# Gated DeltaNet: the first pass's front in 24 fixed slots, and the steps of the triangular inverse 2.7 slots later in each stretch

## The chip, the cores and the metric

The kernel runs on one core of a Trainium2 chip. The metric is device time in microseconds (us), the median of the runs. TensorE (PE in the profile) does the matrix products, VectorE (DVE), ScalarE (ACT) and GpSimd (POOL) do the rest, and SyncE (SP) issues the DMA transfers. Each engine works through its own list of instructions in order.

## The reference, cut to what matters

One inference step of a trunk of two layers: gated DeltaNet (layer 0), then RWKV-7 (layer 1), over 1,104 token rows (64 sample rows, 16 meta tokens, 1,024 prompt tokens). The change touches layer 0 alone. Its core, for each of 16 value heads:

```
proj = xn @ w_in                                  # k, q, v, z and the gate inputs b, a
q, k, v = silu(causal_conv(qkv));  q, k = l2norm(q), l2norm(k)
beta = sigmoid(b);  g = -exp(a_log) * softplus(a + dt_bias);  gc = cumsum(g)
decay = exp(gc[i] - gc[j])                        # causal
L = strict_lower((k*beta) @ k.T * decay);  A = L + I
u, wk = solve(A, v*beta), solve(A, k*beta*exp(gc))      # triangular
v_new = u_c - wk_c @ S                            # chunk after chunk
o = (q*exp(gc)) @ S + (q @ k.T * decay) @ v_new
S = S * exp(g_last) + k_dec.T @ v_new             # state to the next chunk
out = (rmsnorm(o, gn_w) * silu(z)) @ w_out
```

## The kernel before, in words

Layer 0 goes through eight passes j = 0 to 7, each with one key head and its two value heads. A pass has a *front* and a *chain*.

The front makes what doesn't depend on the state: the products k, q and v (tiles `dk`, `dq`, `dv` on TensorE, of xa/xc with the split weights `whi` and `wlo`), the causal convolution (`cvy`, filter taps on DVE, line L520), the SiLU, keys `K`, queries `Q`, value rows `vt` and `bv`; the decay matrices `E` (read from `drow` in DRAM, then exponentials on ACT); the scores of keys with keys; and then the inverse of A. For the inverse the 32 x 32 diagonal blocks of the scores go through DRAM (`ltd`) into one tile of 72 partitions (`invA`); 31 *steps* of two DVE instructions each (`invtmp`, L567, and `invT`, L569) invert all blocks together. `spread` then copies the transposed result on ACT (`invA<-invT`, L737) and sends it through DRAM (`g_t`, `g_u`) into `T1n` (L743) and `TT` (L750). Four *merges* (`rY`, `rU` on TensorE) join blocks of 32 to 64 and to 128.

The chain (`gdn_recur`) takes the state `S` through nine token groups of three units each: `rA` products on TensorE, `X`, `w` and `o`, and the update `S` on DVE (L899). It reads the inverse `TT` of its own pass.

The products run in *slots* of 12 matmuls. A generator, `products()`, yields after each slot, and the 36 slots of a stretch hold k of pass j (6 slots), z of pass j−1 (12), q of pass j (6) and v of pass j (12). Everything else is an *event* with a slot number, put into a table by `gdn_events`, `chain_events` (chain of pass j, from slot `first[j]` on) and `front_events` (front of pass j, by `b` = its stretch's first slot, `qb` = b + 18, and `a` = `first[j]`). `before(u)` calls all events due before slot u. So the chain of pass j−1 and the front of pass j run in the same stretch. On TensorE and ACT the order of the program is the order of execution (`tc.manual_schedule`); on DVE, POOL and SP a scheduler orders the rows by priorities that follow the order of the program.

Before the change pass 0 is an exception: its gates, keys, queries, values, inverse and merges are written out one after the other ahead of slot 0, outside of the manual schedule, and the scheduler orders them on all engines.

The calls that the change speaks of, in `front_events`: `e` is the slot of the first decay, `k` that of the first scores; steps come two at a time in 16 slots from k + 6.6, `spread` at a − 10.3 and the merges at a − 6.5, −4.5, −3.5 and −1.5.

Of the kernel before, what the change touches and what calls it, by code (L numbers as in the profile page):

```python
# [35 lines left out]
class Builder:  # L36
# [308 lines left out]
    def gates(self, xh, xl):  # L345
# [25 lines left out]
        nc.vector.tensor_tensor_scan(gc, sm[32:48], g[32:48], 0.0, op0=ALU.mult, op1=ALU.add)  # L371
        gd = rows[64:80]
# [295 lines left out]
    def gdn_prep(self, j, G):  # L668

        nc, t, gp, fp = self.nc, self.t, self.gp, self.fp  # L670
# [246 lines left out]
    def gdn_events(self, G, open_):  # L917
# [68 lines left out]
    def front_events(self, j, G, b, qb, a, a0, open_):  # L986
# [9 lines left out]
        va, e = qb + 6, max(b + 0.3, a0 - 3.4)  # L996
        k = max(b + 5.5, e + 4.7)
        at(b - 5.7, open_, j)
        at(b - 1.4, lambda: self.history_turn(g().H))
        at(b + 0.1, lambda: self.gdn_prep(j, g()))  # L1000
        for s in range(3):
            at(e + 2 * s, lambda s=s: g().decay(s))
            for tt in range(3):
                at(k + 2 * s - 1.8 + 0.7 * tt, lambda s=s, tt=tt: g().exps(s, tt))
            at(k + 2 * s, lambda s=s: g().scores(s))
            at(qb + (7.6, 16.4, 20.4)[s], lambda s=s: self.gdn_query_norms(g(), s))
        at(k + 4.4, lambda: g().scales())
        at(k + 4.7, lambda: g().blocks())
# [5 lines left out]
        at(b + 11.8, lambda: self.gdn_sample_keys(g(), 0))  # L1014
        at(qb + 4.2, lambda: self.gdn_sample_keys(g(), 1))
        for h, q in ((0, 0), (0, 1), (1, 0)):
            at(b + 13.2, states, h, q)
        at(qb + 6.4, read, 0)
        at(qb + 6.5, states, 1, 1)
        at(qb + 9.9, read, 1)  # L1020
# [1084 lines left out]
    def layer0(self, top, right, xa, xc):  # L2105
# [22 lines left out]
        self.gates(kh, kl)  # L2128
# [6 lines left out]
        def rest(g):  # L2135
            for _ in g:
                pass
        open_(0)
        self.history_turn(G[0].H)
        rest(G[0].keys(0))  # L2140
        self.gdn_zero()
        gates.close()
        self.gp = pool("gdn", ctx)
        g = G[0]
        self.gdn_prep(0, g)
        for s in range(3):
            g.decay(s)
            for tt in range(3):
                g.exps(s, tt)
            g.scores(s)  # L2150
        g.scales()
        g.blocks()
        g.steps(31)
        g.spread()
        rest(self.gdn_queries(0, g, kh, kl, 2048))
        for x in (0, 1):
            self.gdn_sample_keys(g, x)
        for h in (0, 1):
            self.gdn_sample_read(g, h, [self.sample_states(0, h, q) for q in (0, 1)])
        for s in range(3):  # L2160
            self.gdn_query_norms(g, s)
        for h in (0, 1):
            dense = self.gdn_values(0, g, h, kh, kl, (2176, 1152)[h])
            for s in range(3):
                next(dense)
                next(dense)
                self.gdn_value_rows(g, h, s)
            rest(dense)
# [382 lines left out]
```

## Time and profile before

| | |
|---|---|
| median of 3 runs | 2245.91 us (2240.99 to 2247.82) |
| profiled execution: time, span, granted TensorE clock | 2250.41 us, 2248.7 us, 0.968 |
| busy: TensorE, DVE, ACT, POOL | 93%, 71%, 57%, 42% of the span |
| first slot (slot 0) begins | 112.2 us |
| first matmul of chain 0 | 171.5 us |
| a stretch of 36 slots (pass 4) | 526.58 to 652.27: 125.69 us |
| steps of the inverse, all passes (L567 and L569) | 101.3 + 91.3 us of DVE |

A row of a window gives its length, and for TensorE, its weight loads, DVE, ACT and POOL the busy time and the count of instructions, then the granted clock, the DMA share and GB/s. A row of waits gives the total, the times and the longest wait. A row of the timeline gives start, duration, engine, line, operation, output and inputs, shapes and count, and in square brackets the idle time ahead and what ended it. A row of a group ends with busy time, the mean of one in ns, and the idle time ahead of the group.

### The profile page before, as it was taken

The numbers are of one execution on the slowest core, as the hardware profiler recorded it, in microseconds if no ns is written. First come the engines' busy times: TensorE is split into PE (matmuls) and PEld (weight loads), VectorE is DVE, ScalarE is ACT, GpSimd is POOL, SyncE is SP. The second block draws the span as 40 slices with busy tenths as digits, with TensorE's granted clock in tenths as the row PEclk, the third lists the DMA queues.
The fourth block names the chain that finished last, engine by engine and source line by source line (L and its number), as shares of the span: only waits on it lengthen the run. The fifth ranks groups of instructions, "written<-read, shape, count | busy, mean of one in ns | idle before, by whom it ended". The sixth has DMA issues, their size and how long they took to land. (4 is left out here: it accounts for less than half of the span.)

```text
span 2248.7 us, 54824 instructions
## 1 busy us (share of the span) xinstructions
PE 2082.0 (93%) x20404; PEld 1934.5 (86%) x20404; DVE 1586.9 (71%) x4213; ACT 1271.9 (57%) x3641; POOL 941.9 (42%) x1253
## 2 busy tenths in 40 slices
PE   5869899999999999989899999979899999999997
PEld 5859898989898989989799999979798988788886
DVE  7866878788787878876323585676888747766755
ACT  5525556556465656556633365674746546677774
POOL 3533545445353534444323154244533344444444
PEclk9979999999999999999999999989999999999998
DMA  4413332333343333324525314645566375677764
GB/s 119 111 47 85 97 109 80 91 86 98 91 110 79 101 104 86 101 83 117 162 75 139 90 49 150 219 160 179 162 183 174 114 216 162 186 216 226 235 179 137
DMA packets 430661, 292.65 MB, mean 130 GB/s; under 512 B 147145, under 2 KB 412986, under 8 KB 430394
## 3 DMA queue, kind: packets, MB, share of 16 engines
q1 hardware_dynamic: 430394, 289.14, 44.8%
q8 instruction: 161, 2.64, 0.5%
q14 instruction: 106, 0.87, 0.1%
HBM read 197.68 MB, written 91.37 MB: 129 GB/s over the span
## 5 line engine op out<-in xcount | busy, mean ns | idle before, releaser
L90 POOL TENSOR_TENSOR wlo<-wraw,whi 128x512 fp32r<-128x512 f32 (+1 forms) x246 | 336.2, 1368 | 374.8 <-ACT whi L86 321.0
L76 PE MATMUL d<-xc,whi 128*128 128x384 f32 (+2 forms) x1006 | 279.9, 337 | 3.8 <-ACT whi L86 3.8
L520 DVE SCALAR_TENSOR_TENSOR cvy<-raw,cw,cvy 128x408 f32<-128x408 f32 (+2 forms) x288 | 192.1, 667 | 22.8 <-ACT cvy L62 20.6
L86 ACT CAST whi<-wraw 128x512 fp32r<-128x512 f32 (+1 forms) x246 | 149.9, 612 | 91.1 <-PE d L76 52.5
L76 PEld LDWEIGHTS d<-xc,whi 128*128 128x128 f32 (+1 forms) x1006 | 184.4, 190 | 6.0 <-ACT whi L86 4.2
L76 PE MATMUL d<-xc,wlo 128*128 128x384 f32 (+3 forms) x476 | 158.2, 341 | 2.8 <-POOL wlo L90 2.7
L76 PE MATMUL dz<-xc,whi 128*128 128x384 f32 (+1 forms) x480 | 154.8, 340 | 0.0
L76 PE MATMUL dv<-xc,whi 128*128 128x384 f32 (+1 forms) x480 | 152.3, 338 | 0.6 <-ACT whi L86 0.6
L76 PE MATMUL d<-xa,whi 128*128 128x384 f32 (+3 forms) x450 | 143.4, 343 | 3.9 <-DVE xb L1143 2.3
L1086 POOL TENSOR_SCALAR Sb<-Sb,eglb 128x128 f32<-128x128 f32 x128 | 105.3, 839 | 73.2 <-DVE X L877 34.4
L567 DVE TENSOR_TENSOR invtmp<-invA,invT 72x31 f32<-72x31 f32 (+15 forms) x248 | 101.3, 409 | 39.8 <-DMA invA<-ltd 36.0
L62 ACT ACTIVATE o<-rA,gcol 128x128 f32<-128x128 f32 x128 | 42.4, 367 | 147.2 <-DVE S L899 146.8
L76 PE MATMUL dz<-xa,whi 128*128 128x384 f32 (+1 forms) x288 | 99.7, 346 | 0.0
L76 PE MATMUL dv<-xa,whi 128*128 128x384 f32 (+1 forms) x288 | 98.7, 343 | 0.0
L76 PEld LDWEIGHTS d<-xc,wlo 128*128 128x128 f32 (+1 forms) x476 | 89.8, 190 | 7.0 <-POOL wlo L90 4.0
L76 PEld LDWEIGHTS dz<-xc,whi 128*128 128x128 f32 x480 | 90.0, 190 | 4.6 <-issue 4.5
L569 DVE TENSOR_TENSOR invT<-invT,invtmp 72x31 f32<-72x31 f32 (+15 forms) x248 | 91.3, 368 | 3.7
L76 PEld LDWEIGHTS d<-xa,whi 128*128 128x128 f32 (+1 forms) x450 | 85.8, 193 | 7.0 <-issue 4.3
L76 PEld LDWEIGHTS dv<-xc,whi 128*128 128x128 f32 x480 | 89.1, 188 | 2.5 <-issue 1.6
L76 PE MATMUL d<-xa,wlo 128*128 128x384 f32 (+3 forms) x252 | 86.4, 343 | 1.4 <-POOL wlo L90 1.4
L76 PE MATMUL rA<-S,K 128*128 128x128 f32 x256 | 52.1, 308 | 34.9 <-DVE S L899 26.1
L76 PEld LDWEIGHTS rA<-S,K 128*128 128x128 f32 x256 | 41.3, 200 | 44.6 <-DVE S L899 30.4
(523 smaller groups left out, 6963.6 us busy)
## 6 DMA issues: line engine op xcount, KB each, us to landing
wraw<-in_gdn_w_in SPq DMA_DIRECT2D x96, 256.0 KB
wraw<-in_rwkv_w_rkvz SPq DMA_DIRECT2D x80, 256.0 KB
Sb<-in_state_gdn SPq DMA_DIRECT2D x64, 256.0 KB
sldcak<-cakd SPq DMA_DIRECT2D x24, 576.0 KB
wraw<-in_rwkv_w_o SPq DMA_DIRECT2D x42, 256.0 KB
E<-drow SPq DMA_DIRECT2D x24, 384.0 KB
attn<-drow SPq DMA_DIRECT2D x24, 384.0 KB
wraw<-in_gdn_w_out SPq DMA_DIRECT2D x36, 256.0 KB
```

The costliest lines, as they stand in the source:

```text
L62: return self.nc.scalar.activation(out, in_, func, bias=bias, scale=scale, **kw)
L76: self.nc.tensor.matmul(out, lhsT, rhs, start=start, stop=stop)
L86: nc.scalar.copy(hi, x)
L90: e.tensor_tensor(lo, x, hi.bitcast(F32), op=ALU.subtract)
L520: nc.vector.scalar_tensor_tensor(y[0][:, 0:wd], raw[:, k:k + wd], cw[k], y[0][:, 0:wd], op0=ALU.mult, op1=ALU.add)
L567: nc.vector.tensor_tensor(tmp, A[:, j, j + 1:32].unsqueeze(2).broadcast_to([nb, n, m]), Tv[:, j, 0:m].unsqueeze(1).broadcast_to([nb, n, m] ...
L569: nc.vector.tensor_tensor(Tv[:, j + 1:32, 0:m], Tv[:, j + 1:32, 0:m], tmp, op=ALU.subtract)
L1086: self.nc.gpsimd.tensor_scalar(Sb[g][:, u], Sb[g][:, u], self.eglb[:, 2 * j + h, 4 * g + u:4 * g + u + 1], None, op0=ALU.mult)
```

## The change

Three things are changed, and what they compute stays the same.

1. The front of pass 0 gets 24 slots of its own, −24 to −1, within the manual schedule: `products()` begins with k, q and v of pass 0. `gates` becomes a generator whose five later pieces are events at −22.9, −19.4, −16.8, −16.7 and −16.6; decays, exponentials and scores of pass 0 lie at −18.5 to −13.6, its steps three to a slot from −11.5 on, `spread` at −1, and its merges by `first[0]`, as in the other passes.
2. `first` is 9, 43, 78, 114, … where it was 7, 43, 78, 114, …: chain 0 starts two slots later.
3. For the passes 1 to 7 the steps begin at k + 9.3 (15 slots, two steps each) where they began at k + 6.6 (16 slots), and `spread` is at a − 9.9 where it was at a − 10.3.

```diff
@@ gates
             self.act(ya, ya, AF.Exp, scale=-1.0)
+        yield
         xa, ya = x[32:48], y[32:48]
...
         nc.vector.tensor_tensor_scan(gc, sm[32:48], g[32:48], 0.0, op0=ALU.mult, op1=ALU.add)
+        yield
...
         for t3 in range(3):
+            yield
             p = self.ps("f", 2)
@@ gdn_events
-        first = [base[j + 1] + (7 if j < 2 else 6) for j in range(8)]
+        first = [9, 43] + [base[j + 1] + 6 for j in range(2, 8)]
+        for u in (-22.9, -19.4, -16.8, -16.7, -16.6):
+            self.at(u, gate)
+        self.at(-13, swap)
...
-                self.front_events(j, G, base[j], base[j] + 18, first[j], first[j - 1], open_)
+                self.front_events(j, G, base[j], base[j] + 18, first[j], open_, base[j] + max(0.3, first[j - 1] - base[j] - 3.4))
+            else:
+                self.front_events(0, G, -24, -18, first[0], None, None)
@@ front_events
+        if j:
...
+            inv, per, kk, ss, rd = [k + 9.3 + n for n in range(15)], 2, (b + 11.8, qb + 4.2), b + 13.2, (qb + 6.4, qb + 9.9)
+            sp = a - 9.9
+        else:
+            ed, ee, es = [-18.5, -18.4, -18.3], [-16, -15.2, -14.4], [-15.2, -14.4, -13.6]
+            inv, per, kk, ss, rd = [-11.5 + n for n in range(10)], 3, (-12.2, -12.1), -12.8, (-7.6, -4.1)
+            sp = -1
...
-        for n in range(16):
-            at(k + 6.6 + n, lambda: g().steps(2))
-        at(a - 10.3, lambda: g().spread())
+        for u in inv:
+            at(u, lambda: g().steps(per))
+        at(sp, lambda: g().spread())
@@ layer0
-        g.steps(31)
-        g.spread()
-        rest(self.gdn_queries(0, g, kh, kl, 2048))
...
-        for m in g.merges:
-            m()
-        self.last_tokens(0, g.H)
-        self.gdn_events(G, open_)
+        self.gdn_events(G, open_, lambda: next(gate, None), swap)
         def products():
+            yield from G[0].keys(0)
+            yield from self.gdn_queries(0, G[0], kh, kl, 2048)
+            yield from self.gdn_values(0, G[0], 0, kh, kl, 2176)
+            yield from self.gdn_values(0, G[0], 1, kh, kl, 1152)
...
-        before(0)
+        before(-24)
         with tc.manual_schedule(engines={mybir.EngineType.PE, mybir.EngineType.Activation}):
-            self.slot = 0
+            self.slot = -24
```

How the rows stand is best seen at three places. First ACT at the end of the front of pass 0, around the copy of `spread`. Before:

```order
L62 ACTIVATE cvy_1691<-raw_1651,cw_393 128x384
L62 ACTIVATE raw_1607<-cvy_1644 128x408
L86 CAST whi_1735<-wraw_1604 128x512
L544 COPY raw_1720<-dk_1722 128x336
L62 ACTIVATE cvy_1757<-raw_1720,cw_393 128x336
L62 ACTIVATE ktok_1764<-mktok_1762,gcol_123 128x128 x2
L62 ACTIVATE raw_1651<-cvy_1691 128x384
L737 COPY invA_808<-invT_810 72x1024
L62 ACTIVATE TT_11_115<-rU_1453 32x6x32 x2
```

The same place after:

```order
L62 ACTIVATE fss_1336,qeps_1005<-fss_1336 128x128 x3
L547 COPY raw_1317<-dv_1319 128x336
L740 COPY invA_923<-invT_925 72x1024
L62 ACTIVATE cvy_1383<-raw_1317,cw_393 128x336
L62 ACTIVATE raw_1234<-cvy_1293 128x384
L543 COPY raw_1402<-dk_1405 128x8x8
L544 COPY raw_1402<-dk_1405 128x320
L62 ACTIVATE cvy_1463<-raw_1402,cw_393 128x408
```

Before, the copy stood behind all filter work of pass 1's keys (`dk`). Now it stands ahead of the last filter rows of pass 0's own values (`cvy_1383`, and the SiLU `raw_1234`, whose result the next value rows on DVE and then transposes on TensorE take).

Second, DVE in the stretch of pass 4 (526.58 to 652.27 us), where the steps begin; `X`, `S` and `o` belong to the running chain of pass 3. Before:

```order
L877 SCALAR_TENSOR_TENSOR X_7360<-rA_7364,gcol_123,bv_6396 128x128
L1030 SCALAR_TENSOR_TENSOR ovar_7385<-ssq_6937,qeps_6134 128x6
L877 SCALAR_TENSOR_TENSOR X_7361<-rA_7365,gcol_123,bv_6396 128x128
L567 TENSOR_TENSOR invtmp_7339<-invA_7291,invT_7293 72x31
L569 TENSOR_TENSOR invT_7293<-invT_7293,invtmp_7339 72x31
L567 TENSOR_TENSOR invtmp_7342<-invA_7291,invT_7293 72x60
L569 TENSOR_TENSOR invT_7293<-invT_7293,invtmp_7342 72x30x2
L567 TENSOR_TENSOR invtmp_7393<-invA_7291,invT_7293 72x87
```

After:

```order
L880 SCALAR_TENSOR_TENSOR X_7354<-rA_7358,gcol_123,bv_6393 128x128
L1046 SCALAR_TENSOR_TENSOR ovar_7379<-ssq_6937,qeps_6116 128x6
L880 SCALAR_TENSOR_TENSOR X_7355<-rA_7359,gcol_123,bv_6393 128x128
L831 SCALAR_TENSOR_TENSOR zg_7399<-zg_7399,dz_7339 128x384
L110 TENSOR_TENSOR on_t_7382<-ors_7381 128x6
L111 SCALAR_TENSOR_TENSOR on_t_7382<-on_t_7382,ovar_7379 128x6
L112 SCALAR_TENSOR_TENSOR ors_7381<-on_t_7382,ors_7381 128x6
L902 SCALAR_TENSOR_TENSOR S_6936<-S_6936,eglb_124,rA_7358 128x128
L902 SCALAR_TENSOR_TENSOR S_6936<-S_6936,eglb_124,rA_7359 128x128
L570 TENSOR_TENSOR invtmp_7442<-invA_7291,invT_7293 72x31
L572 TENSOR_TENSOR invT_7293<-invT_7293,invtmp_7442 72x31
```

The two rows of `S` that follow `X` now stand ahead of the first step; before they stood behind the sixth.

Third, DVE in the same stretch where the steps end, near the last `S` of the chain. Before:

```order
L899 SCALAR_TENSOR_TENSOR S_6936<-S_6936,eglb_124,rA_7897 128x128
L520 SCALAR_TENSOR_TENSOR cvy_7938<-raw_7871,cw_393,cvy_7938 128x384
L899 SCALAR_TENSOR_TENSOR S_6936<-S_6936,eglb_124,rA_7898 128x128
L567 TENSOR_TENSOR invtmp_8005<-invA_7291,invT_7293 72x31
L910 TENSOR_TENSOR o_7892<-o_7892,rA_7897 128x128
L569 TENSOR_TENSOR invT_7293<-invT_7293,invtmp_8005 72x31
L910 TENSOR_TENSOR o_7892<-o_7892,rA_7898 128x128
```

After:

```order
L570 TENSOR_TENSOR invtmp_8085<-invA_7291,invT_7293 72x87
L572 TENSOR_TENSOR invT_7293<-invT_7293,invtmp_8085 72x3x29
L570 TENSOR_TENSOR invtmp_8088<-invA_7291,invT_7293 72x60
L902 SCALAR_TENSOR_TENSOR S_6936<-S_6936,eglb_124,rA_8011 128x128
L902 SCALAR_TENSOR_TENSOR S_6936<-S_6936,eglb_124,rA_8012 128x128
L572 TENSOR_TENSOR invT_7293<-invT_7293,invtmp_8088 72x2x30
L822 TENSOR_TENSOR bv_8116<-f_8117,sk_6637 128x3x128
L570 TENSOR_TENSOR invtmp_8147<-invA_7291,invT_7293 72x31
L913 TENSOR_TENSOR o_8006<-o_8006,rA_8011 128x128
L913 TENSOR_TENSOR o_8006<-o_8006,rA_8012 128x128
L572 TENSOR_TENSOR invT_7293<-invT_7293,invtmp_8147 72x31
```

Before, the last step stands behind the last but one update `S` of the chain (nine token groups; the last `S` follows 15 rows further on); now it stands behind the last one.

More of the change, by code (lines that the diff above doesn't have):

```diff
@@ L668, in gdn_prep @@
     def gdn_prep(self, j, G):
-        nc, t, gp, fp = self.nc, self.t, self.gp, self.fp
+        nc, t, fp = self.nc, self.t, self.fp
         col = self.col
@@ L995, in read @@
             self.gdn_sample_read(g(), h, [Sb[h, q] for q in (0, 1)])
[L996 to L999, printed above, removed]
+        va = qb + 6
         at(b + 0.1, lambda: self.gdn_prep(j, g()))
+        if j:
+            at(b - 5.7, open_, j)
+            at(b - 1.4, lambda: self.history_turn(g().H))
+            k = max(b + 5.5, e + 4.7)
+            ed, ee, es = [e + 2 * s for s in range(3)], [k + 2 * s - 1.8 for s in range(3)], [k + 2 * s for s in range(3)]
+            inv, per, kk, ss, rd = [k + 9.3 + n for n in range(15)], 2, (b + 11.8, qb + 4.2), b + 13.2, (qb + 6.4, qb + 9.9)
[4 more added lines that the diff above has]
+            sp = -1
@@ L1001, in front_events @@
         for s in range(3):
-            at(e + 2 * s, lambda s=s: g().decay(s))
+            at(ed[s], lambda s=s: g().decay(s))
             for tt in range(3):
-                at(k + 2 * s - 1.8 + 0.7 * tt, lambda s=s, tt=tt: g().exps(s, tt))
-            at(k + 2 * s, lambda s=s: g().scores(s))
+                at(ee[s] + (0.7 if j else 0.25) * tt, lambda s=s, tt=tt: g().exps(s, tt))
+            at(es[s], lambda s=s: g().scores(s))
             at(qb + (7.6, 16.4, 20.4)[s], lambda s=s: self.gdn_query_norms(g(), s))
-        at(k + 4.4, lambda: g().scales())
@@ L1015, in front_events @@
-        at(qb + 4.2, lambda: self.gdn_sample_keys(g(), 1))
+        at(kk[0], lambda: self.gdn_sample_keys(g(), 0))
+        at(kk[1], lambda: self.gdn_sample_keys(g(), 1))
         for h, q in ((0, 0), (0, 1), (1, 0)):
[L1017 to L1020, printed above, removed]
+            at(ss, states, h, q)
+        at(rd[0], read, 0)
+        at(rd[0] + 0.1, states, 1, 1)
+        at(rd[1], read, 1)
         for h in (0, 1):
@@ L2127, in layer0 @@
         rows = [xa[:, k] for k in range(6)] + [xc[:, k] for k in range(10)]
-        self.gates(kh, kl)
+        gate = self.gates(kh, kl)
+        next(gate)
         G = [None] * 8
@@ L2133, in open_, with swap @@
             G[j].H = self.history(j)
-        def rest(g):
-            for _ in g:
-                pass
+        def swap():
+            gates.close()
+            self.gp = pool("gdn", ctx)
         open_(0)
         self.history_turn(G[0].H)
-        rest(G[0].keys(0))
         self.gdn_zero()
[L2142 to L2152, printed above, removed]
-        g.steps(31)
-        g.spread()
-        rest(self.gdn_queries(0, g, kh, kl, 2048))
[L2156 to L2168, printed above, removed]
-        for m in g.merges:
-            m()
-        self.last_tokens(0, g.H)
-        self.gdn_events(G, open_)
+        self.gdn_events(G, open_, lambda: next(gate, None), swap)
         def products():
+            yield from G[0].keys(0)
+            yield from self.gdn_queries(0, G[0], kh, kl, 2048)
+            yield from self.gdn_values(0, G[0], 0, kh, kl, 2176)
+            yield from self.gdn_values(0, G[0], 1, kh, kl, 1152)
             for j in range(1, 8):
```

8 lines of the change are left out of this document (4 added, 4 removed).

## The prediction

> **What bounds the kernel now.** I read the page's first part, then the windows by stage, then who waits for whom, and last the order in time at the places where the change works.
>
> ```profile
> PE 2082.0 (93%) x20404; PEld 1934.5 (86%) x20404; DVE 1586.9 (71%) x4213; ACT 1271.9 (57%) x3641; POOL 941.9 (42%) x1253
> core 0: us, PE busy (x) PEld busy (x) DVE busy (x) ACT busy (x) POOL busy (x), PEclk, DMA share, GB/s
> 112.20:171.50 59.30, 38.94 (x375) 36.17 (x373) 39.40 (x99) 15.44 (x41) 21.12 (x27) 0.71 0.22 54
> 106.22:150.80 44.58, 30.41 (x150) 27.82 (x148) 39.91 (x103) 13.75 (x42) 22.91 (x27) 0.81 0.12 32
> 526.58:652.27 125.69, 119.33 (x1025) 112.83 (x1020) 102.16 (x279) 71.90 (x231) 54.95 (x82) 0.99 0.35 94
> 585.40:641.60 56.20, 50.20 (x370) 47.47 (x369) 49.85 (x136) 30.31 (x103) 27.81 (x40) 0.97 0.28 77
> 590.64:595.82 5.18, 4.94 (x21) 4.75 (x21) 4.96 (x15) 5.18 (x18) 1.28 (x1) 0.67 0.16 41
> 599.05:602.15 3.10, 3.10 (x22) 3.10 (x22) 2.23 (x8) 2.39 (x8) 0.39 (x2) 1.00 0.03 5
> 338.29:343.47 5.18, 4.94 (x20) 4.75 (x21) 4.67 (x16) 4.73 (x18) 0.00 (x0) 0.67 0.01 2
> ```
>
> TensorE is the bound (93%). A steady stretch of 36 slots (526.58:652.27) takes 125.69 us with 119.33 busy, so 6.36 us of it is idle. The end of the front (112.20:171.50) is the one place where TensorE is busy for only 38.94 of 59.30 us, at a granted clock of 0.71. So the change can win in two places: the front, once, and the idle time of the stretches, several times.
>
> The waits name the idle time; the first row below is for 460 to 1031 us (stretches j=3 to 7), the second for 182 to 460 (j=1 and 2), the third for the whole span.
>
> ```profile
> PE rA L76 <- DVE S L899: 20.4, 10, 5.0
> PE rA L76 <- DVE S L899: 5.7, 4, 1.9
> DVE invtmp L567 <- DMA invA<-ltd: 36.0, 8, 6.2
> ```
>
> The first and the third are one story, seen in order of time in the stretch j=4:
>
> ```profile
> 583.81 0.60 PE L76 MATMUL rA<-w,ktok 128*128 128x128 f32 x4
> 585.38 1.25 DVE L567 TENSOR_TENSOR invtmp<-invA,invT 72x31 f32<-72x31 f32 x1 [5.02 <-DMA invA<-ltd]
> 590.25 0.60 DVE L899 SCALAR_TENSOR_TENSOR S<-S,eglb,rA 128x128 f32<-128x128 f32 x2
> 590.64 0.49 PE L76 MATMUL rA<-S,K 128*128 128x128 f32 x2 [3.83 <-DVE S L899]
> 338.29 0.49 PE L76 MATMUL rA<-S,K 128*128 128x128 f32 x2 [1.60 <-DVE S L899]
> ```
>
> VectorE works in its order. Its first inverse step stands at the head and waits 5.02 us for the scores to come back from DRAM. Behind it stand six steps and then the state update S of the running chain, whose inputs were on TensorE at 583.81; S runs at 590.25 and TensorE waits 3.83 us for it. TensorE pays again: after the gap the clock is 0.67 for 5.18 us (590.64:595.82, 21 matmuls), while 22 matmuls take 3.10 us at clock 1.00 (599.05:602.15). I charge 5.18 − 3.10 = 2.1 us. The Trainium skill (TensorE: Matmul & The Clock Gate, "HAM oscillation — how this bites in real kernels") gives the rule "no PE-idle gaps >~3.4µs". By it the short gaps in j=1 and j=2 would cost no clock. The trace disagrees: the gap of 1.60 us at 338.29 is followed by the same 0.67 for 5.18 us (338.29:343.47). By the rule the sum would be about 2 us smaller (half of twice 2.1); I go by the rows.
>
> **The change part by part.**
>
> *Steps 2.7 slots later, stretches j=3 to 7.* In the new order of VectorE the S pair stands ahead of the first step. S could run at about 585.0 (583.81 plus its own matmuls), before the DMA lands at 585.38, so the wait no longer holds it. The possible gain of a stretch is 20.4 / 5 = 4.1 us of stall and 2.1 of clock: 6.2, for five stretches 31. It is not all there to have: the first step can't begin ahead of its transfer, all steps but one still stand ahead of the last S of the chain, and the window between the two gets shorter by whatever is gained.
>
> ```profile
> L567 DVE TENSOR_TENSOR invtmp<-invA,invT 72x31 f32<-72x31 f32 (+15 forms) x248 | 101.3, 409 | 39.8 <-DMA invA<-ltd 36.0
> L569 DVE TENSOR_TENSOR invT<-invT,invtmp 72x31 f32<-72x31 f32 (+15 forms) x248 | 91.3, 368 | 3.7
> 633.40 0.31 SPq L740 DMA_DIRECT2D g_t<-invT  x1
> 636.25 1.43 SPq L743 DMA_DIRECT2D T1n<-g_t  x3
> 641.65 0.61 DVE L899 SCALAR_TENSOR_TENSOR S<-S,eglb,rA 128x128 f32<-128x128 f32 x2 [1.52 <-PE rA L76]
> 643.46 2.13 ACT L737 COPY invA<-invT 72x1024 f32<-72x1024 f32 x1
> 651.02 1.33 PE L76 MATMUL rY<-T1n,E 32*32 32x32 f32 x72
> ```
>
> The steps of a pass cost (101.3 + 91.3) / 8 = 24.1 us. Before, the last one was over at 633.40 (the transfer of its result is issued there); now the last stands right behind S of 641.65. Between 585.40 and 641.60 VectorE is busy for 49.85 us. The first step's 1.25 us was a quarter of it work, and S itself moves ahead, so about 48.25 remain. TensorE's share of that window without stall and slow clock is 56.20 − 6.2 = 50.0. So VectorE would have to run at 96.5%. Where VectorE keeps today's idle time of 56.20 − 49.85 = 6.35 the stretch gains only 56.2 − 54.6 = 1.6 us; where its idle shrinks to 1.75 it gains 6.2. No row decides between them; most of its idle time now is waiting for TensorE, and that shrinks when TensorE doesn't stand. I take the middle, 3.9, times five: 19.5 us (ends 8 and 31).
>
> *Spread and merges.* Spread is issued 0.4 of a slot later; its ACT copy now waits for the last step at about 643.9, where it ran at 643.46 before. Its transfers of g_t, issued at 633.40 before, move to 643.9 and must be back as T1n before rY at 651.02. In the front the same path took (below) 156.39 − 150.78 = 5.6 us, so T1n is there at about 649.7: 1.3 us to spare. I charge nothing; the cover is that 1.3 us. Once it is gone, every later microsecond is a microsecond of TensorE, with 2.1 more for the clock. On SP's queue these DMAs move behind the state loads of that place, which are issued early; on POOL nothing moves past a step.
>
> POOL is the other neighbour: in the new place the steps lie beside its scaling of the sample states.
>
> ```profile
> 622.90 0.45 DVE L567 TENSOR_TENSOR invtmp<-invA,invT 72x175 f32<-72x175 f32 x1
> 623.50 2.43 POOL L1086 TENSOR_SCALAR Sb<-Sb,eglb 128x128 f32<-128x128 f32 x2
> 623.84 0.37 DVE L567 TENSOR_TENSOR invtmp<-invA,invT 72x156 f32<-72x156 f32 x1
> 627.72 1.29 POOL L90 TENSOR_TENSOR wlo<-wraw,whi 128x512 fp32r<-128x512 f32 x1 [1.78 <-ACT whi L86]
> 627.79 1.34 DVE L569 TENSOR_TENSOR invT<-invT,invtmp 72x112 f32<-72x112 f32 x1
> L1086 POOL TENSOR_SCALAR Sb<-Sb,eglb 128x128 f32<-128x128 f32 x128 | 105.3, 839 | 73.2 <-DVE X L877 34.4
> ```
>
> A step beside the scaling at 623.50 took its usual 0.37 us; only the one beside the weight split (627.79) was held, for about 1.0 us. The splits are as many as before, so no charge. The Trainium skill (GPSIMD Engine Reference, "Specifications") says that POOL shares its SBUF interfaces with VectorE and contends with instructions that read two SBUF inputs, as a step does; by it some nine more scalings beside steps, 0.84 us each, would cost VectorE up to 7.6 us a stretch and leave no gain there. The row at 623.84 speaks against it, so it only feeds the third case below.
>
> *j=1 and j=2.* The longest waits there are 1.9 and 1.6 us (the second at 338.29); with 2.1 of clock each that is about 8 in all. Half of it, as above: +4. Against it, chain 0 starts at slot 9 and chain 1 stays at 43, so in j=1 the last S and the merges are two slots nearer; the merges there may wait 2.5 us (between 0 and 5), and in j=2 0.5. Net +1.
>
> *The front of pass 0.* It had been placed by the scheduler; now slots −24 to −1 fix its products, gates and scores on TensorE and ACT.
>
> ```profile
> L520 DVE SCALAR_TENSOR_TENSOR cvy<-raw,cw,cvy 128x408 f32<-128x408 f32 (+2 forms) x288 | 192.1, 667 | 22.8 <-ACT cvy L62 20.6
> 95.01 1.64 DVE L706 SCALAR_TENSOR_TENSOR E<-fsc,bp,E 128x128 f32<-128x128 f32 x6
> 106.22 0.19 DVE L567 TENSOR_TENSOR invtmp<-invA,invT 72x31 f32<-72x31 f32 x1 [4.55 <-DMA invA<-ltd]
> 150.57 0.19 DVE L569 TENSOR_TENSOR invT<-invT,invtmp 72x31 f32<-72x31 f32 x1
> 150.79 1.93 ACT L737 COPY invA<-invT 72x1024 f32<-72x1024 f32 x1 [1.54 <-DVE invT L569]
> 150.78 0.30 SPq L740 DMA_DIRECT2D g_t<-invT  x1
> 156.39 2.71 PE L76 MATMUL rY<-T1n,E 32*32 32x32 f32 x72 [5.81 <-DMA T1n<-g_t]
> 179.88 0.34 PE L76 MATMUL dz<-xc,wlo 128*128 128x384 f32 x1
> 180.06 0.33 PE L76 MATMUL dz<-xc,whi 128*128 128x384 f32 x1
> 180.23 0.61 PE L76 MATMUL rA<-S,K 128*128 128x128 f32 x4
> ```
>
> Scores done at 96.65, first step at 106.22: a path of 9.6 us through DRAM. Then the steps last 44.58 us (106.22:150.80), though they are 24 us of work, because VectorE, busy for 39.91, does other rows among them. The new order has eight fewer of these ahead of the scores' end (four filter taps at 0.67 us, four others at the mean 39.91 / 103 = 0.39: 4.2 us) and sixteen fewer between the first and the last step (eight taps and eight others, 8.5 us). So the last step ends at 150.8 − 4.2 − 8.5 = 138.1 if VectorE is idle for as long as now, and at 133.4 if its 4.7 us of idle go; I take 136. What then stands behind it on TensorE? The transposes of the last value rows, since their SiLU stands behind the ACT copy: a visible wait of some 17 us (from about slot 2, at 122, to 140), longer than any now. From 136 to the end of slot 9: copy, filter and value rows 4.3; eight slots of 12 matmuls, seven at 2.13 (12 x 0.18, the distance of the dz rows) and one at the slow clock, 18.2; merges 7.2; small transposes 2.4; together 32.1, so 168. Before, slot 10 came at 180.23 with 3.7 us of chain work already in it, so 176.5 is its like. Gain 8.4, taken as 8. Ends: −5, where the new order's fixed rows make TensorE and ACT wait for gate pieces, each a chain over ACT, VectorE and DMA; +15, where most of the 17 us wait is filled.
>
> *Sum.* 19.5 + 1 + 8 = 28.5. The profiled execution took 2250.4 us (span 2248.7), so it would be 2222. The median of the runs is 2245.9, 4.5 lower: 2217.5; with a little for what the merges may lose I say 2219.
>
> **The rivals.** 0.3%, about what a measurement of this kernel can tell from no change, is 6.7 us.
>
> A, as forecast: gains of 16 to 38, so 2208 to 2230. Chance 0.50.
>
> B, VectorE has room enough and the stall goes whole: 31 + 1 to 5 + 8 to 12, so 2198 to 2206. For it speaks that VectorE's idle time is made of waits for TensorE; against it the 96.5%. Chance 0.18.
>
> C, VectorE becomes the bound between the first step and the last S: 1 us a stretch, 5, and a front of −1 to +10, so 2231 to 2242. For it speaks the sum of 48.25 in 50.0 us, and what the shared interface would add. Chance 0.14.
>
> D, slower: the steps end after the chain and T1n comes late. Each stretch then pays L − 1.3 for steps ending L later than the 643.9 above, and 2.1 for the clock, against its gain of 6.2. It decides at L of about 5.4; with the front's 8 us the whole kernel breaks even near L = 7. At L = 10, eight of the 24 us of steps behind the chain's S, each stretch loses 4.6, seven stretches 32 less the front's 8 and some of the small stalls: 2260 to 2270. Against it speaks that rows are ordered by slot, and the last step is listed right behind S. Chance 0.11.
>
> E, no change: the wait for the DMA only moves to another place of the same chain, and the front gives what it takes. 2240 to 2252. Against it speaks that S is ahead of the wait. Chance 0.07.
>
> **How the numbers follow.** Likeliest is A: 2219, its own range 2208 to 2230. The range 2198 to 2246 takes in B, C and most of E and leaves out D and tails, under 2 in 10. Faster: A, B and most of C, 0.79. Within 0.3%: most of E and the tail of C, 0.10. Slower: 0.11.
>
> **What the profile after would show.** The wait of rA for S falls from 20.4 us to under 5 in the stretches, which get 3 to 5 us shorter; the wait of invtmp for invA stays, with S ahead of it. A wait of about 17 us of a transpose f for vt in the front, and the first step near 102, the last near 136. If rY waits for T1n in each stretch, D is right; if S is late through all of the chain's second half, C. The prediction is wrong if the front loses: gate pieces that hold TensorE's row before slot −10 would show as waits of f or dq for ACT or VectorE.

## The result and the profile after

The changed kernel takes 2220.1 us (median of 4, 2219.3 to 2220.8), the kernel before 2245.9 (median of 4, 2241.0 to 2247.8): a ratio of 0.9871, interval 0.9849 to 0.9893. The forecast was 2219. The sum came out; its split did not, as the sections below show. One trace is of one execution: it took more than the median of its kernel by 10.4 us in late_steps, 8.7 in norm_late and 11.0 in spread_late, less by 11.9 in fold_before and 7.0 in fold_after, and lies within 5 us of it in the others.

The profiled execution after took 2219.6 us. The page's first lines, and three windows: the rest of the front (113.60:165.80), the stretch j=2 (258.25:390.46) and j=4 (516.77:640.65).

```profile
span 2217.4 us, 54821 instructions
PE 2061.5 (93%) x20404; PEld 1918.7 (87%) x20404; DVE 1572.4 (71%) x4213; ACT 1271.0 (57%) x3641; POOL 952.8 (43%) x1253
113.60:165.80 52.20, 33.93 (x397) 32.02 (x396) 34.66 (x84) 17.33 (x45) 16.53 (x30) 0.80 0.25 61
258.25:390.46 132.21, 123.35 (x1094) 117.39 (x1092) 99.57 (x282) 72.88 (x236) 62.88 (x84) 0.95 0.34 90
516.77:640.65 123.88, 118.51 (x1027) 112.52 (x1021) 96.97 (x279) 71.64 (x231) 57.06 (x82) 0.99 0.35 96
```

POOL is busy for 952.8 us where it was 941.9, with the same 1253 instructions: the one engine that got more expensive. The next table is made from the timelines: the time from the first `dk` matmul of one pass to that of the next, for all runs. "Loop" goes from the first product of pass 0 to the first `dz` behind the stretch j=7, "rest" from there to the end of the span (the last 24 slots with the chain of pass 7, then layer 1), where hardly a row is changed by any of them.

| run | pass 0 | j=1 | j=2 | j=3 | j=4 | j=5 | j=6 | j=7 | loop | rest |
|---|---|---|---|---|---|---|---|---|---|---|
| before | 66.0 | 159.2 | 127.5 | 127.7 | 125.7 | 126.0 | 126.0 | 126.6 | 984.7 | 1217.8 |
| control (before again) | 65.3 | 160.5 | 126.6 | 127.6 | 126.3 | 125.9 | 125.6 | 126.3 | 984.1 | 1215.5 |
| after | 68.3 | 144.7 | 132.2 | 126.3 | 123.9 | 122.7 | 121.8 | 123.8 | 963.7 | 1208.4 |
| late_steps | 66.7 | 162.2 | 131.6 | 130.1 | 124.1 | 124.7 | 124.1 | 122.5 | 986.0 | 1213.0 |
| front_only | 69.0 | 144.7 | 125.8 | 124.1 | 124.9 | 126.4 | 126.0 | 124.6 | 965.5 | 1205.7 |
| first7 | 68.1 | 150.2 | 131.5 | 127.7 | 121.0 | 123.9 | 122.0 | 123.9 | 968.3 | 1211.1 |
| norm_late | 69.1 | 145.2 | 132.6 | 123.6 | 120.5 | 121.4 | 123.3 | 123.4 | 959.2 | 1218.0 |
| mixed | 68.2 | 145.5 | 126.2 | 126.0 | 121.5 | 121.4 | 122.0 | 124.0 | 954.8 | 1203.0 |
| spread_late | 68.5 | 151.3 | 133.2 | 126.7 | 121.1 | 123.4 | 124.3 | 121.9 | 970.4 | 1214.6 |
| no_scaling | 69.3 | 139.9 | 129.6 | 119.9 | 118.0 | 118.7 | 118.4 | 118.1 | 932.1 | 1208.5 |
| fold_before | 66.9 | 155.2 | 124.8 | 123.9 | 120.5 | 121.4 | 120.5 | 119.9 | 953.2 | 1205.6 |
| fold_front_only | 68.2 | 138.5 | 124.8 | 122.6 | 121.8 | 120.5 | 119.9 | 121.2 | 937.5 | 1211.8 |
| fold_mixed | 68.4 | 138.0 | 124.9 | 123.9 | 119.3 | 119.1 | 119.0 | 119.0 | 931.6 | 1211.9 |
| fold_after | 67.9 | 140.5 | 124.4 | 121.0 | 119.4 | 119.1 | 119.1 | 119.2 | 930.5 | 1206.3 |

Two things are to be read from it. The rest varies between 1203 and 1218 us with nearly the same code, so the 9.4 us by which the two profiles differ there need not be the change's. And with the late steps the stretches j=4 to 7 are shorter than before by 1.3 to 5.2 us each, but j=2 is longer by 4 to 6, in every kernel of the upper nine that has them there.

The five stretches j=3 to 7 together, before and after:

```profile
398.91:1030.88 631.97, 599.89 (x5104) 567.46 (x5099) 502.69 (x1396) 359.38 (x1148) 272.94 (x408) 0.98 0.35 95
390.46:1009.02 618.56, 591.49 (x5104) 561.61 (x5100) 490.51 (x1396) 358.14 (x1148) 284.81 (x408) 0.99 0.35 97
```

They are 13.4 us shorter. For the same 5104 matmuls TensorE is busy for 8.4 us less, at a granted clock of 0.99 in place of 0.98, and idle for 5.0 us less. So the larger part came by the clock, the smaller by less idle time.

**Where the waits went.** In the stretches j=3 to 7 (after, 390 to 1009 us), TensorE's two largest waits and the largest of DVE:

```profile
PE rA L76 <- DVE S L902: 12.2, 10, 2.3
PE dv L76 <- POOL wlo L90: 8.2, 5, 1.8
DVE on_t L110 <- POOL ors L102: 27.8, 10, 5.4
```

The wait for S fell from 20.4 to 12.2 us, not to under 5. In the order of time, at the place of j=4 where DVE stood before for `invA`:

```profile
574.39 0.86 POOL L650 TENSOR_SCALAR_AFFINE_SELECT attn<-attn 128x768 f32<-128x768 f32 x1 [9.70 <-PE rA L76]
575.23 1.28 POOL L90 TENSOR_TENSOR wlo<-wraw,whi 128x512 fp32r<-128x512 f32 x1
576.47 1.33 POOL L102 TENSOR_TENSOR ors<-ovar,cvals 128x6 f32<-128x6 f32 x1
571.87 0.56 DVE L831 SCALAR_TENSOR_TENSOR zg<-zg,dz 128x384 f32<-128x384 f32 x1 [1.76 <-ACT zg L62]
577.83 0.17 DVE L110 TENSOR_TENSOR on_t<-ors 128x6 f32<-128x6 f32 x1 [5.41 <-POOL ors L102]
578.32 0.60 DVE L902 SCALAR_TENSOR_TENSOR S<-S,eglb,rA 128x128 f32<-128x128 f32 x2
578.72 0.58 PE L76 MATMUL rA<-S,K 128*128 128x128 f32 x1 [2.27 <-DVE S L902]
578.85 0.18 DVE L570 TENSOR_TENSOR invtmp<-invA,invT 72x31 f32<-72x31 f32 x1
```

S does stand ahead of the first step, as the order said, but three rows of the norm stand ahead of S, and the first of them, `on_t`, waits 5.41 us for `ors`. `ors` is one small power on POOL and stands there behind the mask of `attn` and a weight split. The wait of DVE stayed at about 5 us; only its name changed, from a transfer (the wait of `invtmp` for `invA`, forecast to stay, is gone) to POOL.

POOL itself was not busy there: the mask of `attn` came after 9.70 us of idle time. In two of the five stretches (j=4 and 5) the profile puts that down to a product `rA`, in the three others to the transfer of `attn`, as in j=6:

```profile
820.75 0.86 POOL L650 TENSOR_SCALAR_AFFINE_SELECT attn<-attn 128x768 f32<-128x768 f32 x1 [9.45 <-DMA attn<-drow]
```

So behind POOL's name there mostly stands a transfer again, one queue further back.

The second wait, for `wlo`, was 3.2 us in these stretches before. On POOL, eight scalings of the sample states stand ahead of that split; the lines before (630 to 638 us) and after (617 to 627):

```profile
630.77 3.58 POOL L1086 TENSOR_SCALAR Sb<-Sb,eglb 128x128 f32<-128x128 f32 x4 [1.58 <-PE mktok L73]
634.37 3.00 POOL L1086 TENSOR_SCALAR Sb<-Sb,eglb 128x128 f32<-128x128 f32 x4
637.34 1.28 POOL L90 TENSOR_TENSOR wlo<-wraw,whi 128x512 fp32r<-128x512 f32 x1
```

```profile
617.09 4.41 POOL L1102 TENSOR_SCALAR Sb<-Sb,eglb 128x128 f32<-128x128 f32 x4 [1.51 <-PE rA L76]
621.53 4.21 POOL L1102 TENSOR_SCALAR Sb<-Sb,eglb 128x128 f32<-128x128 f32 x4
625.70 1.29 POOL L90 TENSOR_TENSOR wlo<-wraw,whi 128x512 fp32r<-128x512 f32 x1
627.04 0.44 PE L76 MATMUL dv<-xc,wlo 128*128 128x384 f32 x1 [1.77 <-POOL wlo L90]
```

Eight scalings took 6.58 us before and take 8.62 now, with the late steps on DVE beside them. They are not slowed evenly: two of the eight took 2.21 and 2.28 us (before, 1.54 and 1.25), the others 0.60 to 0.87. It is the same over all 128, before and after (shortest, median and longest in ns):

```profile
L1086 POOL TENSOR_SCALAR Sb<-Sb,eglb x128: 595/620/2554, 107.1 to 1073.1; 128x128 f32<-128x128 f32 x128
L1102 POOL TENSOR_SCALAR Sb<-Sb,eglb x128: 597/660/4043, 101.2 to 1050.9; 128x128 f32<-128x128 f32 x128
```

13 of them took over 1.5 us before and 22 after. Each of these lies beside a dense run of DVE rows on SBUF operands: filter taps, value rows and, in 9 of the 13 and all of the 22, steps.

The front, after: the steps' first and last row, the copy on ACT, the value rows and TensorE's wait.

```profile
98.26 0.18 DVE L570 TENSOR_TENSOR invtmp<-invA,invT 72x31 f32<-72x31 f32 x1
133.91 0.19 DVE L572 TENSOR_TENSOR invT<-invT,invtmp 72x31 f32<-72x31 f32 x1
134.13 1.93 ACT L740 COPY invA<-invT 72x1024 f32<-72x1024 f32 x1 [20.50 <-DVE invT L572]
137.06 0.55 DVE L529 SCALAR_TENSOR_TENSOR vt<-raw,cvy 128x384 f32<-128x384 f32 x1
137.75 0.88 PE L73 MATMUL f<-ident,vt 128*128 128x128 f32 x3 [14.00 <-DVE vt L529]
165.80 0.40 PE L76 MATMUL dz<-xa,whi 128*128 128x336 f32 x1
```

### The profile page after: what moved, and what is told of

Its sections match the earlier page's. It is cut to its first block, busy times and chain, and to the rows that moved or that the text cites. A ratio compares the mean times of both kernels' runs of the same rounds, so it can differ in the third digit from the quotient of the medians.

```text
span 2217.4 us, 54821 instructions
## 1 busy us (share of the span) xinstructions
PE 2061.5 (93%) x20404; PEld 1918.7 (87%) x20404; DVE 1572.4 (71%) x4213; ACT 1271.0 (57%) x3641; POOL 952.8 (43%) x1253
## 5 line engine op out<-in xcount | busy, mean ns | idle before, releaser
L90 POOL TENSOR_TENSOR wlo<-wraw,whi 128x512 fp32r<-128x512 f32 (+1 forms) x246 | 326.2, 1328 | 363.0 <-ACT whi L86 324.7
L523 DVE SCALAR_TENSOR_TENSOR cvy<-raw,cw,cvy 128x408 f32<-128x408 f32 (+2 forms) x288 | 186.2, 647 | 26.9 <-ACT cvy L62 25.1
L1102 POOL TENSOR_SCALAR Sb<-Sb,eglb 128x128 f32<-128x128 f32 x128 | 119.5, 949 | 74.9 <-DMA Sb<-in_state_gdn 28.0
L76 PE MATMUL dq<-xc,whi 128*128 128x384 f32 (+1 forms) x240 | 78.7, 345 | 3.0 <-ACT whi L86 3.0
L76 PE MATMUL dk<-xc,whi 128*128 128x384 f32 (+1 forms) x240 | 78.8, 348 | 0.0
```

The source lines that it names most:

```text
L76: self.nc.tensor.matmul(out, lhsT, rhs, start=start, stop=stop)
L90: e.tensor_tensor(lo, x, hi.bitcast(F32), op=ALU.subtract)
L523: nc.vector.scalar_tensor_tensor(y[0][:, 0:wd], raw[:, k:k + wd], cw[k], y[0][:, 0:wd], op0=ALU.mult, op1=ALU.add)
L1102: self.nc.gpsimd.tensor_scalar(Sb[g][:, u], Sb[g][:, u], self.eglb[:, 2 * j + h, 4 * g + u:4 * g + u + 1], None, op0=ALU.mult)
```

## The experiments

**The parts alone.** Four kernels ran together, all against the kernel before.

late_steps, the third edit on the old front:

```diff
-        for n in range(16):
-            at(k + 6.6 + n, lambda: g().steps(2))
-        at(a - 10.3, lambda: g().spread())
+        for n in range(15):
+            at(k + 9.3 + n, lambda: g().steps(2))
+        at(a - 9.9, lambda: g().spread())
```

> The kernel before with the third edit alone: steps from k + 9.3 in 15 slots, spread at a - 9.9; the old front and first = 7 stay. Theory (each edit pays by itself, and the late steps pay 1.4 to 4.2 us in each of the stretches j=3 to 7, 13.4 in all, and cost 4 to 5 us in j=2): 2235 to 2240 us, stretches j=3 to 7 at 122 to 126.5 us, the wait of rA for S at 2.0 to 2.3 in each, j=2 at about 132. Rival (the loss in j=2 comes from chain 0 that starts two slots later): j=2 stays at 127.5 and the kernel takes 2231 to 2234. Rival (the stretches gain only together with the new front): 2244 to 2248.

Measured: 2236.7 us, ratio 0.9945 (0.9923 to 0.9967). The time is as expected, and j=2 took 131.6 us, so the rival that blames the later chain 0 for j=2 is out. Not as expected, j=3 took 130.1 us (122 to 126.5), and the loop of the trace is no shorter than before (986.0 against 984.7). The trace lies 10.4 us above the median, so its stretches say little on the size of the gain.

front_only, the first two edits with the old steps:

```diff
-            inv, ... = [k + 9.3 + n for n in range(15)], ...
-            sp = a - 9.9
+            inv, ... = [k + 6.6 + n for n in range(16)], ...
+            sp = a - 10.3
```

> The changed kernel with the steps of the passes 1 to 7 back at k + 6.6 in 16 slots and spread back at a - 10.3; the 24 slots of the front and first = 9 stay. Theory: the front and the stretch j=1 keep their 13 us, j=3 to 7 go back to 125.7 to 127.7 us with a wait of rA for S of 3.5 to 5, j=2 goes back to about 127.5: 2231 to 2234 us. Rival (chain 0 at slot 9 is what costs j=2): j=2 stays at 132 and the kernel takes 2235 to 2239.

Measured: 2221.5 us, 0.9892 (0.9866 to 0.9917), 10 us faster than expected. The new front and first = 9 alone bring nearly all: 24.3 of the 25.8 us by the medians. The intervals of this kernel and the changed one overlap, so on the new front the late steps can't be told from no change. j=1 came as expected; j=2 took 125.8 and j=3 124.1 us, where some 127.5 and 125.7 to 127.7 were expected, and the rest of the program was short. Two rows tell the old from the new steps here, the waits in j=3 to 7 and the scaling's group:

```profile
PE rA L76 <- DVE S L902: 18.1, 10, 3.9
PE dv L76 <- POOL wlo L90: 3.2, 5, 0.7
L1102 POOL TENSOR_SCALAR Sb<-Sb,eglb 128x128 f32<-128x128 f32 x128 | 105.6, 840 | 78.0 <-DMA Sb<-in_state_gdn 52.0 <-DVE X L880 6.8 <-PE fss L73 6.7
```

With the steps at the old place the scaling takes 840 ns as before, and TensorE waits more for S and less for `wlo`. In the changed kernel the same group reads:

```profile
L1102 POOL TENSOR_SCALAR Sb<-Sb,eglb 128x128 f32<-128x128 f32 x128 | 119.5, 949 | 74.9 <-DMA Sb<-in_state_gdn 28.0 <-DVE X L880 27.6 <-PE rA L76 9.2
```

control, no edit:

> The kernel before once more, for its trace: the two profiles differ by 31.3 us in span, the medians by 25.8, and 9.4 us of the difference of the profiles lie behind the last stretch, where nothing was changed. Theory (those are differences between two executions of the same code, in DMA waits): 2242 to 2248 us, and the part from 1009/1031 us to the end is 4 to 9 us shorter than in the first profile. Rival (the tail really gained, since it starts in another state of the queues): the tail is as long as in the first profile.

Measured: 2248.4 us, 1.0011 (0.9991 to 1.003). Its rest was 1215.5 us, only 2.3 shorter than in the first profile, so this one execution is nearer to the rival. But late_steps has 1213.0 and norm_late, with the new front, 1218.0: old front or new, the rest varies over a range that covers both, and the rival is not borne out either.

first7, chain 0 back at slot 7:

```diff
-        first = [9, 43] + ...
+        first = [7, 43] + ...
```

> The changed kernel with first[0] = 7 in place of 9: chain 0, its spread-dependent merges and what hangs on them two slots earlier. Theory (TensorE waits for the last step anyway, and fewer slots are left to run ahead of the merges): the front loses 1 to 5 us, j=1 and j=2 get back 1 to 5 us since chain 0 ends two slots earlier: 2217 to 2224 us, the wait in the front 14 to 20 us. Rival (j=2's loss is the chain's two slots): j=2 goes back to 127.5 and the kernel takes 2214 to 2217.

Measured: 2225.4 us, 0.9899 (0.987 to 0.9928), 1 us above the range expected. j=1 took 150.2 instead of 144.7 us and j=2 131.5 instead of 132.2: by these traces the two slots are worth about 5 us in j=1 and cost j=2 nothing. The medians say 5 us too, but the intervals of the two kernels overlap. The rival is out.

**What holds S, wlo and the front.** These four ran together on the changed kernel.

norm_late:

```diff
-        self.rsqrt(rs, vv, gp, "on")
+        newton = self.rsqrt(rs, vv, gp, "on", later=True)
+        def late():
+            with self.tc.issue_after(self.anchor):
+                newton()
+        if s:
+            newton()
+        else:
+            self.at(u, late)
...
-            nm[s] = self.gdn_norm(j, G[j], s, *G[j].seg[s])
+            nm[s] = self.gdn_norm(j, G[j], s, *G[j].seg[s], a + 10.1)
```

> The changed kernel, and in each pass the first group's three small DVE rows on_t, on_t, ors (the Newton step of the norm's reciprocal root) are held back until the state update S ahead of them is issued, so that they stand behind the pair of S and not ahead of it. Theory (in the changed kernel S of this place waits behind on_t, which waits 5.4 us for POOL's ors, as it waited for the transfer of invA before): the wait of rA for S in the stretches j=3 to 7 falls from 2.0 - 2.3 us to under 0.7, each of them gets 2 to 4 us shorter, 2204 to 2213 us. Rival (S is late for another reason, TensorE's own w products): wait and time stay, 2218 to 2222. Rival (the wait moves to the norm's scaled copies on ACT, which come later): ACT's wait for ors grows and the time stays.

Measured: 2215.7 us, 0.9867 (0.9845 to 0.9889); loop 959.2, that is 4.5 shorter. The waits in j=3 to 7:

```profile
PE rA L76 <- DVE o L913: 10.2, 11, 1.9
PE dv L76 <- POOL wlo L90: 7.9, 5, 1.8
PE rA L76 <- DVE S L902: 2.1, 5, 0.4
```

S is no longer waited for (2.1 us in place of 12.2), so `on_t` was what held it. About half of that came back as a wait for `o`, the next rows behind `on_t` (10.2 in place of 4.8). The time of 2215.7 is between theory and rival, and its interval overlaps that of the changed kernel.

mixed, the late steps in the passes 4 to 7 alone:

```diff
-            inv, ... = [k + 9.3 + n for n in range(15)], ...
+            inv, ... = [k + 9.3 + n for n in range(15)] if j >= 4 else [k + 6.6 + n for n in range(16)], ...
-            sp = a - 9.9
+            sp = a - (9.9 if j >= 4 else 10.3)
```

> The changed kernel with the steps of the passes 1 to 3 at their old place (k + 6.6, spread at a - 10.3) and of the passes 4 to 7 at the new one. Theory (late steps cost 6 us in j=2 and 2 in j=3 and pay 1 to 4 in each of j=4 to 7): the loop of slots is 6 to 9 us shorter than in the changed kernel, 2211 to 2216 us. Rival (what j=2 and j=3 show in single profiles is chance): 2219 to 2222.

Measured: 2206.1 us, 0.9831 (0.9812 to 0.9849), 5 us below the range expected; loop 954.8, that is 8.9 shorter, as expected, 6.0 of it in j=2, which took 126.2. This beats both kernels, and shows that j=2's loss under late steps is no chance.

no_scaling:

```diff
     def gdn_sample_scale(self, j, h, Sb):
-        for g in (0, 1):
+        for g in ():
             for u in range(4):
                 self.nc.gpsimd.tensor_scalar(Sb[g][:, u], ...)
```

> The changed kernel without POOL's scaling of the sample states by the decay in the chains (128 instructions L1102 of 0.95 us; it leaves out that factor of the sample states' update). Theory (the later steps lie beside this scaling, POOL is slowed by them, 0.95 against 0.84 us, and comes late with the weight split wlo): the wait of dv for wlo of 1.1 to 3.9 us a stretch falls under 0.7, the stretches j=2 to 7 get 1.5 to 4 us shorter, 2203 to 2212 us. Rival (wlo is late because of ACT's whi ahead of it, not of POOL): the wait stays, 2217 to 2221.

This kernel leaves out the decay of the sample states. Measured: 2182.7 us, 0.9727 (0.9706 to 0.9749): 37 us less than the changed kernel, where 8 to 17 were expected. Both waits are gone or nearly so from j=3 to 7 (`wlo` isn't among them at all):

```profile
PE rA L76 <- DVE o L913: 4.5, 8, 0.8
PE rA L76 <- DVE S L902: 1.6, 5, 0.3
```

So POOL's scaling was behind the late `wlo` and behind the late S as well. For S the traces suggest a way, which was not tested by itself. SyncE's queue in j=4 of the changed kernel:

```profile
562.53 1.06 SPq L1114 DMA_DIRECT2D out_s_gdn<-Sb  x2
567.24 3.15 SPq L715 DMA_DIRECT2D ltd<-E  x4
570.43 0.44 SPq L646 DMA_DIRECT2D attn<-drow  x1
```

The scaled states are written out ahead of the last scores and of the transfer of `attn`, on which the mask, `ors`, `on_t` and S hang. Counted from the first `dk` of the stretch, `attn<-drow` is issued at 53.7 us here, at 50.1 without the scaling and at 51.9 with the fold below. One stretch doesn't fit: j=2 still took 129.6 us, without any wait for `wlo`; with the fold and the same steps it took 124.4.

spread_late:

```diff
-            sp = -1
+            sp = 1.5
```

> The changed kernel with spread of pass 0 at slot 1.5 in place of -1: ACT's copy stands behind the filter rows of slots -1 to 1 and no longer holds the last value rows. Theory (the 14 us that TensorE waits in the front are the steps' own length on DVE, and the value rows are only what stands at the gate): the wait of f for vt goes and a wait of rY for T1n of 8 to 16 us takes its place, and the time stays within 3 us: 2217 to 2223. Rival (the copy on ACT is what holds TensorE): most of the 14 us is won, 2206 to 2212 us.

Measured: 2220.8 us, 0.9902 (0.988 to 0.9924). The time stayed and the wait got another name, as the theory had it. At 17.79 us the wait is longer than the 8 to 16 expected, and j=1 took 151.3 us in this trace, 6.6 more than in the changed kernel. The first row of the merges:

```profile
145.17 0.31 PE L76 MATMUL rY<-T1n,E 32*32 32x32 f32 x2 [17.79 <-DMA T1n<-g_t]
```

The 14 us of TensorE in the front are the length of the steps on DVE, whatever row stands at the gate.

**The scaling taken off POOL.** The fold computes the same: the decay of the sample states goes into the add that DVE makes anyway.

```diff
     def gdn_sample_scale(self, j, h, Sb):
-        ... gpsimd.tensor_scalar(Sb[g][:, u], Sb[g][:, u], self.eglb[...], None, op0=ALU.mult)
+        pass
     def gdn_sample_write(self, j, h, G, Sb):
-            nc.vector.tensor_tensor(x, x, ps, op=ALU.add)
+            for u in range(4):
+                nc.vector.scalar_tensor_tensor(Sb[g][:, u], Sb[g][:, u], self.eglb[:, hv, 4 * g + u:4 * g + u + 1],
+                                               ps[:, 128 * u:128 * u + 128], op0=ALU.mult, op1=ALU.add)
```

> The changed kernel with the decay of the sample states folded into the add that writes them: 128 scalings on POOL (0.95 us each) and 32 adds of 512 columns on DVE (0.68 us) become 128 rows of 128 columns on DVE (scaled add, 0.30 to 0.35 us), with the same result. Theory (POOL's scaling is what keeps the changed kernel's stretches at 122 to 132 us; DVE has room for 16 us more in all): 2180 to 2192 us, stretches j=3 to 7 at 118 to 121 us, the waits of dv for wlo and of rA for S under 0.7. Rival (the load only moves to DVE, which becomes the bound): 2205 to 2220, with rA waiting for S.

> The same fold with the new front, and the steps of the passes 1 to 7 at the old place. Theory (what the later steps won at the wait for S, POOL's slower scaling took away again; without scaling on POOL the later steps are worth what was forecast of them, 2 to 4 us a stretch): 10 to 20 us slower than the changed kernel with the fold, 2195 to 2208 us, with rA waiting for S behind invA's transfer for 2.5 to 4 us in each of j=3 to 7. Rival (POOL's load itself is the cost, and the place of the steps matters little with it or without): within 5 us of the other.

> The same fold with the new front, old steps in the passes 1 to 3 and late ones in 4 to 7. Theory (j=2's loss under late steps is POOL's): 0 to 6 us slower than with late steps throughout, 2184 to 2196. Rival (j=2 loses by late merges, POOL or not): 2 to 5 us faster.

> The kernel before with the fold. Theory (with the old steps the scaling was not slowed, 0.84 us, and S waited for invA's transfer, which the fold doesn't touch): 5 to 20 us faster than before, 2225 to 2240. Rival (POOL's load costs the same in both kernels): 30 to 38 us faster, 2208 to 2216.

| kernel | without the fold | with the fold | ratio with the fold to before |
|---|---|---|---|
| before | 2245.9 | 2218.5 | 0.9875 (0.9845 to 0.9905) |
| front_only | 2221.5 | 2196.6 | 0.9782 (0.9758 to 0.9806) |
| after | 2220.1 | 2191.0 | 0.9762 (0.9733 to 0.9791) |
| mixed | 2206.1 | 2185.8 | 0.9732 (0.9706 to 0.9758) |

In fold_after the wait for S in j=3 to 7 is 2.6 us and `wlo` is not waited for:

```profile
PE rA L76 <- DVE o L913: 4.9, 10, 0.7
PE rA L76 <- DVE S L902: 2.6, 10, 0.3
```

fold_after came as its theory had it. For fold_before the rival was nearer: 27 us faster, not 5 to 20. POOL's scaling was dear in the old order too. The theory had said that the fold doesn't touch the transfer of `invA`, but DVE's wait for it fell from 36.0 to 23.7 us, and with it TensorE's wait for S in j=3 to 7, from 20.4 to 4.3 us, though no step was moved:

```profile
DVE invtmp L567 <- DMA invA<-ltd: 23.7, 8, 4.8
PE rA L76 <- DVE S L899: 4.3, 13, 1.1
```

The late steps are worth 5.6 us with the fold by the medians (2196.6 to 2191.0; loop 7.0) and 1.4 without it (loop 1.8). Neither is clear of noise: the intervals overlap in both pairs. With the fold that is below the 10 to 20 us of the theory and nearer to its rival, and the wait of 2.5 to 4 us for S in each stretch, which the theory had for the old steps, wasn't there: 6.5 us in all in j=3 to 7, 1.6 the longest. fold_mixed took 2185.8 against the 2191.0 of fold_after (the intervals overlap), the number of its rival, but not by j=2: with the fold j=2 takes 124.4 to 124.9 us with either steps. It is the fastest of the kernels that compute the whole.

## Why the prediction was right, step by step

**The front: the mechanism right, the size near.** Forecast were a first step near 102, a last near 136 and a wait of f for vt of 17 us to 140; they were at 98.26 and 133.9, and the wait was 14.00 us to 137.75. Slot 10 was forecast at 168 and came at 165.8 (against the like of 176.5: 10.7 us, forecast 8.4). At the end of j=1 the gain stood at 13.2 us, against the 8 and part of the 1 forecast; by the trace of first7 about 5 us of j=1 come from chain 0's two slots, which I had booked as a loss of 2.5 (merges nearer to the last S).

**What front_only brings beyond it isn't explained.** Its loop is 19.2 us shorter than before's, but pass 0 and j=1 make only 11.5 of it: j=2, j=3 and j=7 are 1.7, 3.6 and 2.0 us shorter though their steps stand where they stood. In j=2 and j=3 most of it is the clock: granted were 1.00 in both, where before it was 0.99 and 0.97, and TensorE was busy for 1.2 and 2.7 us less. Why the clock stayed up there was not tried.

**The term of the stretches j=3 to 7 was mis-sized.** "3.9, times five: 19.5": by the profiles it was 13.4, of it 1.4 in j=3 and 1.8 to 4.2 in each of j=4 to 7. And not all of that is the late steps': front_only, with the old steps, already has 6.0 of it (625.97 us). The late steps then made 7.4 in j=3 to 7 and lost 6.4 in j=2. The step that failed is "so the wait no longer holds it": I checked that S had come ahead of the first step, and not what else had come ahead of S. `on_t` was in the order shown, ahead of S, but its releaser, POOL's `ors`, I did not look up. norm_late shows it. The room of VectorE was not the limit: from the first step of j=4 to the last S (578.85 to 630.20) it was busy for 45.68 of 51.35 us, 89% and not 96.5%. Nor did the merges pay: in j=3 to 7 no wait of `rY` for `T1n` is listed.

**"The splits are as many as before, so no charge" was wrong.** I asked of the shared neighbourhood of steps and scaling only whether the steps get slower (0.37 us beside a scaling, so no). That was right: all steps took 192.6 us before and 193.3 after. It is the scaling that got slower, 839 to 949 ns on average and 6.58 to 8.62 us for the eight ahead of a split; late_steps (977 ns) and front_only (840 ns) tell that it is the steps' place that does it. The Trainium skill (GPSIMD Engine Reference, "Specifications") says that POOL shares its SBUF interfaces with VectorE, with contention where a VectorE instruction has two SBUF inputs; these rows agree with it, on POOL's side of the contention, which I had not priced. TensorE paid with 8.2 us of waiting for `wlo` where it was 3.2.

**j=1 and j=2: net +1 was forecast; j=2 lost 4.7 us.** Its wait for `wlo` grew from 2.4 to 3.9 us, which is the same step, but the larger part is the clock: 0.95 in that window above, where it was 0.99, and TensorE was busy for 3.7 us more. With the old steps (mixed) and with the fold (fold_after) the loss is gone. In no_scaling 2.1 us of it stay, with no wait for `wlo` and at a clock of 0.95 too, so what slows the clock in j=2 is open.

**The clock's 2.1 us is no fixed price.** Two gaps of about the same length in the changed kernel, 2.27 us (at 578.72) and 2.20 (at 702.58), were followed by these:

```profile
578.72:583.90 5.18, 5.18 (x24) 4.89 (x25) 4.08 (x16) 5.18 (x18) 1.28 (x1) 0.69 0.11 28
702.58:707.76 5.18, 4.88 (x33) 4.69 (x34) 4.63 (x17) 5.18 (x18) 1.30 (x1) 1.00 0.17 45
```

The first ran at 0.69 and the second at full clock, 33 matmuls against 24 in the same time. So shorter gaps may go without the price. By the rule of 3.4 us that the prediction cites from the Trainium skill (TensorE: Matmul & The Clock Gate, "HAM oscillation — how this bites in real kernels") both would have gone without it, and one did not.

**The sum was right by compensation.** In the loop, −13.2 to the end of j=1, +4.7 in j=2 and −13.4 in j=3 to 7 make −21.9 between the profiles (this counts from the start of the span); forecast were −28.5. The remaining 9.4 of the 31.3 us of span are spread over the rest, which varies that much by itself. The medians say −25.8. By edits it is further from the forecast. The terms gave the first two edits 8 − 3 = 5 us and the late steps 19.5 + 4 = 23.5; measured are 24.3 for the first two, and for the late steps 9 on the old front and 1.4 on the new one. The parts do not simply add, and why is open. That two errors of some 20 us cancelled is luck.

## What to carry to other kernels

When a row is moved ahead of the one that waits, look up the releaser of every row that now stands ahead of the freed one: a queue has only one head, and the next late row takes its place. Then look at the queue of that releaser too: here `ors` stood behind a mask that waited for a transfer. Ask of two engines side by side which of them gets slower, on both sides. An engine that is busy for 42% of the span can be behind several waits that carry other names: take its work away once, and see which names vanish.

## What the runs showed of the hardware that was not expected

POOL's 128x128 scaling takes 0.60 to 0.70 us in most places (80 of 128 before, 73 after). Beside a dense run of DVE rows on SBUF operands single ones take 1.5 to 4.0 us, 13 of them before and 22 after, which moves the mean from 0.84 to 0.95 us; the DVE rows beside them keep their time (taps 0.55 to 0.64 us, steps 0.21 to 0.44). And 128 such scalings, 105 us of POOL's 942, were worth 20 to 29 us of a kernel that is bound by TensorE, when DVE took them over for 15.1 us more of its own time in the changed kernel (1572.4 to 1587.5 us busy) and 2.9 in the kernel before (1586.9 to 1589.8).
